# A decoder layer on one core: a second product in the first sweep over x, and the last attention groups placed between other blocks

## The chip, the cores and the metric

The kernel runs on one core of a Trainium2 chip. The metric is the device time of one execution in microseconds (us), and lower is better. Before the change the median of three runs is 1527.37 us (1514.87 to 1532.27).

## The reference, cut to what matters

One layer of a decoder with 256 tokens and 2048 channels, in fp32. It has three sub-layers: token mixing, attention into 256 memory tokens, and a gated MLP with a short convolution. The MLP takes the larger half of the time. The change touches token mixing alone:

```python
proj = x @ w_in[l]
(sq, sk, sv, gq, gk, gv, gz, gb, ga, gate_swa, gate_gdn) = split_columns(proj, IN_WIDTHS)
y_swa = swa_attention(sq, sk, sv, swa_sinks[l], rel_bias) @ w_br_swa[l]       # 16 heads, window 128
y_gdn = gated_deltanet(gq, gk, gv, gz, gb, ga, ...) @ w_br_gdn[l]             # 8 heads of 128
mixed = sigmoid(gate_swa) * y_swa + sigmoid(gate_gdn) * y_gdn
...
z = silu(gz).reshape(b, s, GDN_HEADS, GDN_HEAD_DIM)   # in gated_deltanet: 1024 columns of z
o = o * rsqrt(mean(o*o) + 1e-6) * norm_w
return (o * z)
```

The delta rule also needs, for each head, a short causal convolution with SiLU over k, q and v, and a matrix of decays `exp(gc_i - gc_j)` from the cumulated gates.

## The kernel before, in words

**Numbers.** Each fp32 operand is split into a high and a low part (`split`, L60: ScalarE writes the high part, VectorE subtracts), and each product is made of hi*hi, hi*lo and lo*hi. So every weight that lands from memory passes through ScalarE (`whi`, L61) and VectorE (`wlo`, L58) before TensorE may use it. Weights arrive in tiles `raw` of up to 1024 columns on the sync queue (`load_raw`, L64 to L67). There are four buffers each of `raw`, `whi` and `wlo`. `load_w` (L69) gives its load and split a higher priority than the code around it, by 40 places or another number (`ahead`).

**Two forms of product.** `prod_a` (L81) keeps the weights stationary and streams x: 16 k-tiles, each a matmul of 512 columns and one of 256. One block of 128 output channels is 32 matmuls from two raw tiles. `prod_b` (L97) keeps x stationary and streams the weights: per k-tile and half of the tokens three matmuls of n columns. It can be called for a part of the k-tiles (`k_from`, `k_to`) and go on into the same PSUM tiles (`ps`).

**Order of the work.** Tile, the framework, puts each engine's instructions into one list, by the order of the program and the priorities; each engine then runs its list in that order. The first part of the program is:

- L158 to L160: eight matmuls on zeros.
- L186 to L189, the first k sweep: for six ranges of k-tiles (1, 1, 2, 4, 4, 4) `load_x` loads x (on ScalarE's queue, L169) and splits it, and `prod_b` multiplies it with `wS`. Those 400 columns are v of the attention, the two gates and the first 256 columns of z.
- L312 to L317: blocks of the attention's k and q with `prod_a`, the position bias through GpSimd's DMAs, scores and softmax of head group 0 (`swa_probs(0)`).
- L319 to L341: cumulated gates, a DMA that spreads them over the partitions (`dgd`, `dcr`), and the decays: 16 VectorE instructions (L339) and 16 exponentials on ScalarE (L340, L341).
- L343 to L357: head groups 1 to 3 of the attention in turn with the rest of z: `wZ0` (512 columns) in two halves of k, and `wZ1` (256 columns). `swa_probs(g)` makes scores in four PSUM banks and the softmax; `swa_out(g)` makes 12 transposes of the probabilities (L300), three copies (L301), 6 matmuls with v (L306) and two splits (L310). The banks of these steps come from one pool of four (`bank`, tag `sm`); the products use another pool of four (tag `mm`).
- L428 to L434: the delta rule's heads, three blocks each for k, q and v (`gdn_block`, L381: a `prod_a`, the convolution on VectorE, SiLU), and the scores of the head before.

After that come the triangular inverse on VectorE beside the attention's output products, the merge, the memory attention and the MLP.

Of the kernel before, what the change touches and what calls it, by code (L numbers as in the profile page):

```python
# [14 lines left out]
P = 128  # L15
# [18 lines left out]
def tile_layer(ctx: ExitStack, tc: tile.TileContext, a, out):  # L34
# [19 lines left out]
    def stt(o, i0, s, i1, op0, op1, **k):  # L54
        nc.vector.scalar_tensor_tensor(o, i0, s, i1, op0=op0, op1=op1, **k)  # L55
# [36 lines left out]
    def evac_a(ps, dst):  # L92
        hl = tp.tile([P, T], F32, tag="hl", name="hl")
        nc.scalar.copy(hl, ps[:, T:])  # L94
        tt(dst, ps[:, :T], hl, ALU.add)

    def prod_b(w, kt, n, xs, tail=0, ps=None, k_from=0, k_to=None, ahead=AHEAD, homes={}):  # L97
        pss = ps or [pb.tile([P, 512], F32, tag="mm", name="mm") for _ in range(2)]
        step = min(kt, U // n)
        pend = []  # L100

        def emit(items, order):
            for h in order:
                for kk, wh, wl in items:
                    o = pss[h][:, :n]
                    xh, xl = xs(kk, h)
                    mm(o, xh, wh, kk == 0, False)
                    mm(o, xh, wl, False, False)
                    mm(o, xl, wh, False, kk == kt - 1)

        for k0 in range(k_from, k_to or kt, step):
            ks = min(step, (k_to or kt) - k0)
            wh, wl = load_w(w[:, k0 * n:(k0 + ks) * n], ks, n, ahead, homes.get(k0))
            for k in range(ks):
                it = (k0 + k, wh[:, k, :], wl[:, k, :])
                if it[0] >= kt - tail:
                    pend.append(it)
                else:
                    emit([it], (0, 1))
        if pend:  # L120
            emit(pend, (0, 1))
        return pss

    def halves(x):
        def f(kk, h):
            v = x(kk)
            return v[:, 0, h * P:(h + 1) * P], v[:, 1, h * P:(h + 1) * P]
        return f
# [37 lines left out]

    def load_x(k0, n):
        raw = xst[k0 // 8].rearrange("p q (k t) -> p (q k) t", t=T)[:, k0 % 8:k0 % 8 + n, :]
        nc.scalar.dma_start(raw, a["xT"][:, k0 * T:(k0 + n) * T].rearrange("p (k t) -> p k t", t=T))  # L169
        x, c = xhl[k0 // 8], slice(k0 % 8, k0 % 8 + n)  # L170
        split(x[:, c, 0, :], x[:, c, 1, :], raw)

# [7 lines left out]
    def z_gate(c0, n, h, src):  # L180
        zc = zn[:, h, c0:c0 + n]
        nc.scalar.activation(zc, src, AF.Silu)
        z3 = zc.rearrange("p (h d) -> p h d", d=P)
        tt(z3, z3, nrm.unsqueeze(1).broadcast_to([P, n // P, P]), ALU.mult, nc.gpsimd)

    pss = None  # L186
    for k0, n in ((0, 1), (1, 1), (2, 2), (4, 4), (8, 4), (12, 4)):
        load_x(k0, n)
        pss = prod_b(a["wS"], KT, 400, halves(xs), ps=pss, k_from=k0, k_to=k0 + n, ahead=20)  # L189
    nc.sync.dma_start(sml, a["sml"].partition_broadcast(P))  # L190
    nc.sync.dma_start(cst, a["cst"])
    nc.sync.dma_start(nrm, a["nrm"].partition_broadcast(P))
# [1 line left out]
        nc.scalar.copy(svg[:, h, :], ps[:, :144])  # L194
    for h, ps in enumerate(pss):
        z_gate(0, 256, h, ps[:, 144:400])


    rd = dp.tile([16, RELW], F32, name="rd")
# [8 lines left out]
    def sm16(name):  # L208
        return cp.tile([P, 2, 8], F32, name=name)
# [49 lines left out]
    def swa_probs(g):  # L259
        b = biasg[g // 2][:, 4 * (g % 2):4 * (g % 2) + 4, :]  # L260
        s = S[:, g % 2]
        s0, s1 = s[:, :, 0:128], s[:, :, 128:384]
        for j in range(2):
            r = slice(64 * j, 64 * j + 64)
            hh = slice(2 * j, 2 * j + 2)
            for sd, bd, tq, nk in ((s1, b, slice(128, 256), 256), (s0, b[:, :, 128:256], slice(0, 128), 128)):
                ps = bank()[:, :2 * nk].rearrange("p (h k) -> p h k", k=nk)
                for i in range(2):
                    q = qhl[r, g % 2, i, :, tq]
                    mm(ps[:, i, :], q[:, 0, :], khl[r, 0, :nk], True, False)  # L270
                    mm(ps[:, i, :], q[:, 0, :], khl[r, 1, :nk], False, False)
                    mm(ps[:, i, :], q[:, 1, :], khl[r, 0, :nk], False, True)
                stt(sd[:, hh, :], ps, 0.125, bd[:, hh, :], ALU.mult, ALU.add)
        mx = tp.tile([P, 2, 4], F32, tag="mx", name="mx")
        nc.vector.reduce_max(mx[:, 0, :], s0, axis=AX.X)
        nc.vector.reduce_max(mx[:, 1, :], s1, axis=AX.X)
        sk = sinkb[:, 4 * g:4 * g + 4].unsqueeze(1).broadcast_to([P, 2, 4])
        tt(mx, mx, sk, ALU.max)
        nm = tp.tile([P, 2, 4], F32, tag="nm", name="nm")
        nc.vector.tensor_scalar_mul(nm, mx, -1.0)  # L280
        l = tp.tile([P, 2, 4], F32, tag="l", name="l")
        for h in range(4):
            nc.scalar.activation(s0[:, h, :], s0[:, h, :], AF.Exp, bias=nm[:, 0, h:h + 1],
                                 accum_out=l[:, 0, h:h + 1])
            nc.scalar.activation(s1[:, h, :], s1[:, h, :], AF.Exp, bias=nm[:, 1, h:h + 1],
                                 accum_out=l[:, 1, h:h + 1])
        tt(mx, sk, nm, ALU.add)
        nc.scalar.activation(mx, mx, AF.Exp)
        tt(l, l, mx, ALU.add)
        nc.vector.reciprocal(l, l)  # L290
        for bl, sd in ((0, s0), (1, s1)):
            tt(sd, sd, l[:, bl, :].unsqueeze(2).broadcast_to(list(sd.shape)), ALU.mult)

    def swa_out(g):
        s = S[:, g % 2]
        pt = slot(f"E{4 + g % 2}", [P, 4, RELW], F32, "pt")
        for c in range(3):
            ps = bank()
            for h in range(4):
                pe_t(ps[:, h * P:(h + 1) * P], s[:, h, c * P:(c + 1) * P])  # L300
            nc.scalar.copy(pt[:, :, c * P:(c + 1) * P], ps.rearrange("p (h k) -> p h k", k=P))  # L301
        po = bank().rearrange("p (b i q) -> p b i q", b=2, i=2)
        for bl, c, t, st, sp_ in ((0, 0, 0, True, True), (1, 1, 0, True, False), (1, 2, 1, False, True)):
            for j in range(2):
                r = slice(64 * j, 64 * j + 64)
                mm(po[r, bl], sv[:, t, r], pt[:, 2 * j:2 * j + 2, c * P:(c + 1) * P], st, sp_)  # L306
        o = osT[g // 2][:, 2 * (g % 2):2 * (g % 2) + 2]
        for bl in range(2):
            q = slice(bl * P, bl * P + P)
            split(o[:, :, 0, q], o[:, :, 1, q], po[:, bl])  # L310
# [22 lines left out]
    dcr = e8[:, 3:7, :].rearrange("p a (b t) -> p (a b) t", t=P)  # L333
    nc.gpsimd.dma_start(dgd, gd.partition_broadcast(P))
    nc.gpsimd.dma_start(dcr, gd[1].partition_broadcast(P))
    for h in range(8):
        for hf in range(2):
            d = dgd[:, hf, h, :]
            stt(d, d, ngc[:, hf, h:h + 1], msk, ALU.add, ALU.add)  # L339
        nc.scalar.activation(dcr[:, h, :], dcr[:, h, :], AF.Exp, bias=suf[:, 0, h:h + 1])  # L340
        nc.scalar.activation(dgd[:, :, h, :], dgd[:, :, h, :], AF.Exp)  # L341

    swa_q(2)  # L343
    zps = prod_b(a["wZ0"], KT, 512, halves(xs), k_to=8)
    swa_probs(1)
# [4 lines left out]
        z_gate(256, 512, h, zps[h])  # L350
    swa_probs(2)
    swa_out(1)
    for h, ps in enumerate(prod_b(a["wZ1"], KT, 256, halves(xs))):
        z_gate(768, 256, h, ps[:, :256])
    swa_probs(3)
    swa_out(2)
    swa_out(3)  # L357

    def transpose_split(src, kt, dst):
# [6 lines left out]
            split(hi, lo, ps)  # L366


    nc.sync.dma_start(gcw, a["gcw"])
    nc.sync.dma_start(fcw, a["fcw"])  # L370
    nc.sync.dma_start(lnT, a["lnT"])
    cvr = []
    for i in range(3):
        c = cp.tile([P, 3 + T], F32, name=f"cv{i}")
        nc.vector.memset(c[:, 0:3], 0.0)
        cvr.append(c)

    ua = [slot(f"T{i}", [P, 4, 768], F32, f"ua{i}") for i in range(2)]
    vp = slot("E1", [P, 2, 8, P], F32, "vp")
    ks, ck, sq, cq = sm16("ks"), sm16("ck"), sm16("sq"), sm16("cq")  # L380
    def gdn_block(h, j, dst):  # L381
        blk = 3 * h + j
        cv = cvr[blk % 3]
        evac_a(prod_a(a["wA"][blk], xs), cv[:, 3:])
        ca = tp.tile([P, T], F32, tag="ca", name="ca")
        nc.vector.tensor_scalar_mul(ca, cv[:, 3:3 + T], gcw[:, blk, 3:4])
        for w in (2, 1, 0):
            stt(ca, cv[:, w:w + T], gcw[:, blk, w:w + 1], ca, ALU.mult, ALU.add)
        nc.scalar.activation(dst, ca, AF.Silu)

    def gdn_scores(h, kq, vt):
        kh = tp.tile([P, 2, T], F32R, tag="t2", name="kh", bufs=3)
        kl = tp.tile([P, 2, T], F32R, tag="t2", name="kl", bufs=3)
# [31 lines left out]
        for hf in range(2):  # L425
            nc.scalar.activation(vp[:, hf, h, :], ps[:, hf * P:(hf + 1) * P], AF.Copy,
                                 scale=sq[:, hf, h:h + 1])
    kqv = slot("E6", [P, 2, 3, T], F32, "kqv")  # L428
    for h in range(8):
        for j in range(3):  # L430
            gdn_block(h, j, kqv[:, h % 2, j, :])
            if j == 0 and h:
                gdn_scores(h - 1, kqv[:, (h - 1) % 2, 0:2, :], kqv[:, (h - 1) % 2, 2, :])
    gdn_scores(7, kqv[:, 1, 0:2, :], kqv[:, 1, 2, :])  # L434
# [436 lines left out]
```

## Time and profile before

| | us |
|---|---|
| median of three runs | 1527.37 |
| lowest, highest | 1514.87, 1532.27 |
| the profiled execution | 1521.04 |
| its span, first to last instruction | 1519.3 |
| TensorE busy in it | 1497.7 |

A profile shows one execution. TensorE has two rows, PE for matmuls and PEld for the loading of the stationary operand. An engine's busy time counts overlapping instructions once. A wait names the instruction that ended it. "Clock" is the share of TensorE's full clock that was granted.

### The profile page before, as it was taken

What the parts mean: (1) busy time and instruction counts of PE and PEld (TensorE: products, weight loads), DVE (VectorE), ACT (ScalarE), POOL (GpSimd) and SP (SyncE); (2) the same over time, 40 slices, a digit from 0 to 9 for tenths busy, and PEclk for the clock granted to TensorE, in tenths of its full rate; (3) what the DMA queues carried; (4) which work ended last, traced back from release to release, by engine and by line L of the source; (5) the groups of instructions that cost most, each with busy time, mean ns of one, the idle gap of its engine ahead of it and who ended that gap; (6) DMA issues with size and microseconds to landing.
All of it is one profiled execution on the core that took longest, in us unless ns stands there. A gap on an engine that the chain in (4) does not pass through costs nothing.

```text
span 1519.3 us, 21775 instructions
## 1 busy us (share of the span) xinstructions
PE 1497.7 (99%) x8182; PEld 1279.1 (84%) x8182; DVE 1094.2 (72%) x1803; ACT 749.3 (49%) x1153; POOL 57.0 (4%) x93
## 2 busy tenths in 40 slices
PE   7999999999999999999999999999999999999998
PEld 6878888888898888888878888888888888888886
DVE  4876888869956666659579777887777787455455
ACT  5566654554446555436455454444445444343332
POOL 0101002030001000000000000000000000000000
PEclk9999999999999999999999999999999999999999
DMA  7853455585554656765644555555555557666663
GB/s 255 229 177 124 153 171 178 169 241 191 186 192 144 190 190 192 246 189 169 219 139 153 191 191 187 192 187 193 190 190 191 188 192 242 195 196 192 187 203 118
DMA packets 79845, 285.75 MB, mean 188 GB/s; under 512 B 9659, under 2 KB 10876, under 8 KB 78460
## 3 DMA queue, kind: packets, MB, share of 16 engines
q1 hardware_dynamic: 75404, 267.55, 54.9%
q0 software_dynamic: 3040, 14.06, 3.0%
q10 hardware_dynamic: 1296, 2.75, 0.5%
q8 instruction: 64, 1.05, 0.3%
q14 instruction: 41, 0.34, 0.1%
HBM read 281.80 MB, written 2.52 MB: 187 GB/s over the span
## 4 chain that ended last, share of the span: by engine, by line
PE 67%; DVE 1%; ACT 0%; POOL 0%; issue 0%; DVEq 0%
PE mm L46 66%; PE sm L46 1%; PE sm L151 1%; DVE wlo L58 0%; POOL rv L58 0%; DVE xn L55 0%; DVE st L617 0%; ACT whi L61 0%; DVE xn L592 0%; DVE zn L55 0%; DVE xn L58 0%; ACT xn L590 0%; DVE x2hl L58 0%; ACT ptm L677 0%; DVE mv L577 0%
## 5 line engine op out<-in xcount | busy, mean ns | idle before, releaser
L58 DVE TENSOR_TENSOR wlo<-raw,whi 128x1024 fp32r<-128x1024 f32 (+3 forms) x505 | 611.9, 1213 | 299.0 <-ACT whi L61 297.0
L61 ACT CAST whi<-raw 128x1024 fp32r<-128x1024 f32 (+3 forms) x505 | 526.5, 1044 | 575.8 <-PE mm L46 417.6
L46 PE MATMUL mm<-x2hl,whi 128*128 128x512 f32 x1376 | 477.6, 394 | 0.6 <-DVE x2hl L58 0.6
L46 PE MATMUL mm<-x2hl,wlo 128*128 128x256 f32 x1376 | 381.3, 277 | 0.0
L46 PE MATMUL mm<-xhl,whi 128*128 128x512 f32 x1040 | 369.1, 398 | 0.0
L46 PEld LDWEIGHTS mm<-x2hl,whi 128*128 128x128 f32 x1376 | 257.9, 188 | 60.6 <-DVE x2hl L58 0.8
L46 PE MATMUL mm<-xhl,wlo 128*128 128x256 f32 x1040 | 290.8, 280 | 0.0
L46 PEld LDWEIGHTS mm<-x2hl,wlo 128*128 128x128 f32 x1376 | 258.2, 188 | 0.1
L46 PEld LDWEIGHTS mm<-xhl,whi 128*128 128x128 f32 x1040 | 195.3, 188 | 47.8 <-issue 2.4
L46 PEld LDWEIGHTS mm<-xhl,wlo 128*128 128x128 f32 x1040 | 196.0, 188 | 0.0
L46 PE MATMUL mm<-whi,hT_E 128*128 128x512 f32 x384 | 119.3, 389 | 0.0
L46 PE MATMUL mm<-whi,hT_T 128*128 128x512 f32 x288 | 89.4, 389 | 0.0
L55 DVE SCALAR_TENSOR_TENSOR ca<-cv,fcw,ca 128x256 f32<-128x256 f32 x172 | 83.0, 482 | 4.3
L46 PEld LDWEIGHTS mm<-whi,hT_E 128*128 128x128 f32 x384 | 72.1, 188 | 15.1
L46 PE MATMUL mm<-whi,mixT 128*128 128x512 f32 x256 | 79.0, 389 | 0.0
L46 PE MATMUL mm<-wlo,hT_E 128*128 128x512 f32 x192 | 74.7, 389 | 0.0
L94 ACT COPY hl<-mm 128x256 f32<-128x256 f32 x191 | 68.8, 360 | 0.0
L46 PEld LDWEIGHTS mm<-whi,hT_T 128*128 128x128 f32 x288 | 54.1, 188 | 11.3
L46 PE MATMUL mm<-whi,xhl 128*128 128x400 f32 (+2 forms) x192 | 51.9, 352 | 7.0 <-ACT xhl L61 6.4
L58 DVE TENSOR_TENSOR cv<-mm,hl 128x256 f32<-128x256 f32 x110 | 46.0, 418 | 15.1 <-ACT hl L94 15.1
L46 PEld LDWEIGHTS mm<-whi,mixT 128*128 128x128 f32 x256 | 48.0, 188 | 10.0
L46 PE MATMUL mm<-wlo,hT_T 128*128 128x512 f32 x144 | 56.0, 389 | 0.0
(254 smaller groups left out, 1604.3 us busy)
## 6 DMA issues: line engine op xcount, KB each, us to landing
raw<-in_wU_dram SPq DMA_DIRECT2D x172, 512.0 KB, 4.4
raw<-in_wD_dram SPq DMA_DIRECT2D x84, 512.0 KB, 4.3
raw<-in_wA_dram SPq DMA_DIRECT2D x66, 512.0 KB, 4.0
raw<-in_wGS_dram SPq DMA_DIRECT2D x32, 512.0 KB, 4.3
raw<-in_wGG_dram SPq DMA_DIRECT2D x32, 512.0 KB, 4.4
raw<-in_wMO_dram SPq DMA_DIRECT2D x32, 512.0 KB, 4.4
raw<-in_wBS_dram SPq DMA_DIRECT2D x16, 512.0 KB, 4.1
raw<-in_wBG_dram SPq DMA_DIRECT2D x16, 512.0 KB, 4.3
```

What stands on the lines that cost most here:

```text
L46: nc.tensor.matmul(o, l, r, start=start, stop=stop)
L55: nc.vector.scalar_tensor_tensor(o, i0, s, i1, op0=op0, op1=op1, **k)
L58: (eng or nc.vector).tensor_tensor(o, i0, i1, op=op)
L61: nc.scalar.copy(dst_hi, src)
L94: nc.scalar.copy(hl, ps[:, T:])
L151: nc.tensor.transpose(o, i, ident)
```

## The change

- The first k sweep takes nine ranges of k-tiles (1, 1, 2, then six of 2). After each range of the `wS` product the same range of the `wZ1` product is made, into two PSUM tiles of its own. The two tiles of the `wS` product come from the pool `sm`. The product `wZ1` between the attention groups is gone.
- The loads of x are issued on the sync queue.
- `swa_probs(3)` comes behind `swa_out(1)`; then the k and q blocks of the delta rule's first head, `swa_out(2)`, its v block, and `swa_out(3)`.
- The 16 + 16 instructions of the decays stand behind the first head's k and q blocks in the program.

```diff
     def load_x(k0, n):
-        nc.scalar.dma_start(raw, a["xT"][:, k0 * T:(k0 + n) * T].rearrange("p (k t) -> p k t", t=T))
+        nc.sync.dma_start(raw, a["xT"][:, k0 * T:(k0 + n) * T].rearrange("p (k t) -> p k t", t=T))
...
-    pss = None
-    for k0, n in ((0, 1), (1, 1), (2, 2), (4, 4), (8, 4), (12, 4)):
+    pss = [bank() for _ in range(2)]
+    zps = [pb.tile([P, 512], F32, tag="mm", name="mm") for _ in range(2)]
+    for k0, n in ((0, 1), (1, 1), (2, 2), (4, 2), (6, 2), (8, 2), (10, 2), (12, 2), (14, 2)):
         load_x(k0, n)
-        pss = prod_b(a["wS"], KT, 400, halves(xs), ps=pss, k_from=k0, k_to=k0 + n, ahead=20)
+        prod_b(a["wS"], KT, 400, halves(xs), ps=pss, k_from=k0, k_to=k0 + n, ahead=20)
+        prod_b(a["wZ1"], KT, 256, halves(xs), ps=zps, k_from=k0, k_to=k0 + n, ahead=20)
...
+    for h, ps in enumerate(zps):
+        z_gate(768, 256, h, ps[:, :256])
...
-    for h in range(8):
-        for hf in range(2):
-            d = dgd[:, hf, h, :]
-            stt(d, d, ngc[:, hf, h:h + 1], msk, ALU.add, ALU.add)
-        nc.scalar.activation(dcr[:, h, :], dcr[:, h, :], AF.Exp, bias=suf[:, 0, h:h + 1])
-        nc.scalar.activation(dgd[:, :, h, :], dgd[:, :, h, :], AF.Exp)
-
     swa_q(2)
...
     swa_out(1)
-    for h, ps in enumerate(prod_b(a["wZ1"], KT, 256, halves(xs))):
-        z_gate(768, 256, h, ps[:, :256])
     swa_probs(3)
-    swa_out(2)
-    swa_out(3)
...
+    kqv = slot("E6", [P, 2, 3, T], F32, "kqv")
+    gdn_block(0, 0, kqv[:, 0, 0, :])
+    gdn_block(0, 1, kqv[:, 0, 1, :])
+    for h in range(8):
+        for hf in range(2):
+            d = dgd[:, hf, h, :]
+            stt(d, d, ngc[:, hf, h:h + 1], msk, ALU.add, ALU.add)
+        nc.scalar.activation(dcr[:, h, :], dcr[:, h, :], AF.Exp, bias=suf[:, 0, h:h + 1])
+        nc.scalar.activation(dgd[:, :, h, :], dgd[:, :, h, :], AF.Exp)
+
+    swa_out(2)
+    gdn_block(0, 2, kqv[:, 0, 2, :])
+    swa_out(3)
...
     for h in range(8):
         for j in range(3):
-            gdn_block(h, j, kqv[:, h % 2, j, :])
+            if h:
+                gdn_block(h, j, kqv[:, h % 2, j, :])
```

What the lists of the engines look like is shown at three places. First the start of the sync engine's list, which issues the loads of `raw` and now those of x; before:

```order
L66 DMA raw<-in_wS_dram 128x400 x2
L66 DMA raw<-in_wS_dram 128x800 x4
L190 DMA sml<-in_sml_dram 128x32
L66 DMA raw<-in_wS_dram 128x800 x3
L191 DMA cst<-in_cst_dram 128x512
L66 DMA raw<-in_wA_dram 128x1024
```

and after the change:

```order
L66 DMA raw<-in_wS_dram 128x400
L66 DMA raw<-in_wZ_dram 128x256
L66 DMA raw<-in_wS_dram 128x400
L169 DMA xst_104<-in_xT_dram 128x256
L66 DMA raw<-in_wZ_dram 128x256
L169 DMA xst_104<-in_xT_dram 128x256
L169 DMA xst_104<-in_xT_dram 128x512
L66 DMA raw<-in_wS_dram 128x800
L66 DMA raw<-in_wZ_dram 128x512
```

The loads of x stand among those of the weights, x of the first k-tile fourth, and nothing else is issued ahead of the last range; `cst` and the first `wA` tile follow behind it.

Second the decays in VectorE's list (`dgd`), among the low parts of the weights (`wlo`); before:

```order
L58 TENSOR_TENSOR wlo<-raw,whi 128x1024
L55 SCALAR_TENSOR_TENSOR dgd<-dgd,ngc,cst 128x128 x16
L58 TENSOR_TENSOR wlo<-raw,whi 128x1024
L58 TENSOR_TENSOR qk<-mm,hl 128x256
L58 TENSOR_TENSOR wlo<-raw,whi 128x1024
```

and after:

```order
L58 TENSOR_TENSOR wlo<-raw,whi 128x1024
L58 TENSOR_TENSOR qhl<-qk,qhl 128x256
L55 SCALAR_TENSOR_TENSOR dgd<-dgd,ngc,cst 128x128 x3
L58 TENSOR_TENSOR wlo<-raw,whi 128x1024
L55 SCALAR_TENSOR_TENSOR dgd<-dgd,ngc,cst 128x128 x7
L58 TENSOR_TENSOR wlo<-raw,whi 128x1024
L55 SCALAR_TENSOR_TENSOR dgd<-dgd,ngc,cst 128x128 x6
```

The 16 instructions stand in three pieces with a `wlo` between them, and start two `wlo` later.

Third TensorE's list from the end of `swa_out(1)` (`sm<-pt,swakv`) on; before, `wZ1` followed, here its first rows:

```order
L151 MATMUL sm<-cst,S 128x128 x12
L46 MATMUL sm<-pt,swakv 64x256 x6
L46 MATMUL mm<-whi,xhl_102 128x256
L46 MATMUL mm<-wlo,xhl_102 128x256
L46 MATMUL mm<-whi,xhl_102 128x256 x2
```

and now the scores of group 3 (`sm<-khl,qhl`) follow, and then 64 matmuls of two delta-rule blocks, of which the first two are shown:

```order
L46 MATMUL sm<-pt,swakv 64x256 x6
L46 MATMUL sm<-khl,qhl 128x256 x6
L46 MATMUL sm<-khl,qhl 128x128 x6
L46 MATMUL sm<-khl,qhl 128x256 x6
L46 MATMUL sm<-khl,qhl 128x128 x6
L46 MATMUL mm<-xhl_102,whi 128x512
L46 MATMUL mm<-xhl_102,wlo 128x256
```

Behind those 64 come the 12 transposes of `swa_out(2)`.

## Rows read from the trace of the kernel before

**Rows 1.** The page, part 1: busy us (share of the span) xinstructions.
```profile
PE 1497.7 (99%) x8182; PEld 1279.1 (84%) x8182; DVE 1094.2 (72%) x1803; ACT 749.3 (49%) x1153; POOL 57.0 (4%) x93
```
**Rows 2.** Windows; columns: stretch, length, busy by engine, clock, DMA share, GB/s.
```profile
0.00:34.40 34.40, 25.79 (x107) 21.39 (x107) 16.94 (x26) 16.99 (x23) 0.20 (x4) 0.95 0.78 254
34.40:165.00 130.60, 126.71 (x760) 105.77 (x760) 94.45 (x167) 82.03 (x180) 14.12 (x19) 0.97 0.56 172
165.00:1519.30 1354.30, 1345.17 (x7319) 1151.94 (x7317) 982.84 (x1612) 650.32 (x952) 42.67 (x70) 1.00 0.59 188
```
**Rows 3.** Waits from 0 to 34 us: total us, times, longest.
```profile
ACT xhl L61 <- DMA xst<-in_xT_dram: 10.3, 4, 5.7
...
PE mm L46 <- ACT xhl L61: 6.4, 4, 3.0
```
**Rows 4.** Timeline of PE: start us, us, instruction, count [idle before].
```profile
5.16 0.54 PE L46 MATMUL mm<-whi,xhl 128*128 128x400 f32 x1
...
25.08 0.63 PE L46 MATMUL mm<-whi,xhl 128*128 128x400 f32 x2 [0.63 <-DVE xhl L58]
...
33.62 0.81 PE L46 MATMUL sm<-oh,ohr 33*16 33x384 f32 x2
34.36 0.50 PE L46 MATMUL mm<-xhl,whi 128*128 128x512 f32 x1
...
62.82 1.38 PE L46 MATMUL sm<-khl,qhl 64*128 64x256 f32 x11
```
**Rows 5.** Timeline of ACT, its DMA queue: the last load of x.
```profile
15.93 0.34 ACTq L169 DMA_DIRECT2D xst<-in_xT_dram  x1
```
**Rows 6.** DMA issues from 0 to 30 us: count, KB each, median us to landing.
```profile
raw<-in_wS_dram SPq DMA_DIRECT2D x7, 400.0 KB, 5.6
...
xst<-in_xT_dram ACTq DMA_DIRECT2D x3, 512.0 KB, 8.6
raw<-in_wS_dram SPq DMA_DIRECT2D x2, 200.0 KB, 3.5
```
**Rows 7.** Windows, columns as in rows 2: a starved stretch of the first sweep.
```profile
15.00:20.00 5.00, 2.98 (x8) 2.54 (x9) 2.18 (x2) 1.04 (x1) 0.00 (x0) 0.69 0.91 301
```
**Rows 8.** Groups by shape, 0 to 34 us: busy us, mean ns | idle before.
```profile
L58 DVE TENSOR_TENSOR wlo<-raw,whi 128x800 fp32r<-128x800 f32 x7 | 6.7, 987 | 1.7 <-ACT whi L61 1.7
...
L58 DVE TENSOR_TENSOR xhl<-xst,xhl 128x512 fp32r<-128x512 f32 x1 | 0.7, 693 | 2.4 <-ACT xhl L61 2.4
...
L61 ACT CAST whi<-raw 128x1024 fp32r<-128x1024 f32 x3 | 3.2, 1051 | 2.9 <-DMA raw<-in_wA_dram 1.7 <-PE mm L46 1.1
```
**Rows 9.** Timeline of PE: `wZ1` begins, and `swa_out(2)` with what follows it.
```profile
129.63 0.38 PE L46 MATMUL mm<-whi,xhl 128*128 128x256 f32 x1
...
141.34 0.50 PE L46 MATMUL sm<-khl,qhl 64*128 64x256 f32 x2
...
145.18 0.66 PE L151 MATMUL sm<-cst,S 128*128 128x128 f32 x4 [0.23 <-DVE S L55]
```
**Rows 10.** Waits of PE from 34 to 165 us: total us, times, longest.
```profile
PE sm L151 <- DVE S L55: 2.5, 3, 1.2
PE mm L46 <- DVE wlo L58: 1.3, 1, 1.3
```
**Rows 11.** Timeline of DVE: the decays' 16 instructions.
```profile
79.33 4.29 DVE L55 SCALAR_TENSOR_TENSOR dgd<-dgd,ngc,cst 128x128 f32<-128x128 f32 x16 [0.76 <-DMA dgd<-gd]
```
**Rows 12.** Timelines of ACT and DVE behind `swa_out(1)`.
```profile
130.15 1.28 ACT L283 ACT_TABLE_LOAD   x1
...
135.07 0.34 ACT L61 CAST osT<-sm 128x256 fp32r<-128x256 f32 x1
...
135.81 1.82 DVE L58 TENSOR_TENSOR S<-S,l 128x512 f32<-128x512 f32 x2
```
**Rows 13.** Windows, columns as in rows 2: around `swa_out(0)` and `swa_out(1)`.
```profile
81.00:99.00 18.00, 15.54 (x84) 11.23 (x83) 14.65 (x27) 10.09 (x21) 0.00 (x0) 0.91 0.61 194
121.00:130.00 9.00, 7.88 (x53) 5.55 (x52) 6.22 (x10) 3.95 (x8) 2.51 (x2) 0.81 0.40 130
```

More of the change, by code (lines that the diff above doesn't have):

```diff
@@ L352, in tile_layer @@
     swa_out(1)
-    for h, ps in enumerate(prod_b(a["wZ1"], KT, 256, halves(xs))):
-        z_gate(768, 256, h, ps[:, :256])
     swa_probs(3)
-    swa_out(2)
-    swa_out(3)
-    def transpose_split(src, kt, dst):
-        for k0 in range(0, kt, 2):
-            ps = bank().rearrange("p (k t) -> p k t", t=T)
-            for k in range(2):
-                for h in range(2):
-                    pe_t(ps[:, k, h * P:(h + 1) * P], src(k0 + k, h))
-            hi, lo = dst(k0)
-            split(hi, lo, ps)
     nc.sync.dma_start(gcw, a["gcw"])
@@ L376, in tile_layer @@
         cvr.append(c)
-    ua = [slot(f"T{i}", [P, 4, 768], F32, f"ua{i}") for i in range(2)]
-    vp = slot("E1", [P, 2, 8, P], F32, "vp")
     ks, ck, sq, cq = sm16("ks"), sm16("ck"), sm16("sq"), sm16("cq")
@@ L389, in gdn_block, with transpose_split @@
         nc.scalar.activation(dst, ca, AF.Silu)
+    kqv = slot("E6", [P, 2, 3, T], F32, "kqv")
[10 more added lines that the diff above has]
+    swa_out(3)
+    def transpose_split(src, kt, dst):
+        for k0 in range(0, kt, 2):
+            ps = bank().rearrange("p (k t) -> p k t", t=T)
+            for k in range(2):
+                for h in range(2):
+                    pe_t(ps[:, k, h * P:(h + 1) * P], src(k0 + k, h))
+            hi, lo = dst(k0)
+            split(hi, lo, ps)
+    ua = [slot(f"T{i}", [P, 4, 768], F32, f"ua{i}") for i in range(2)]
+    vp = slot("E1", [P, 2, 8, P], F32, "vp")
     def gdn_scores(h, kq, vt):
@@ L427, in gdn_scores @@
                                  scale=sq[:, hf, h:h + 1])
-    kqv = slot("E6", [P, 2, 3, T], F32, "kqv")
     for h in range(8):
         for j in range(3):
-            gdn_block(h, j, kqv[:, h % 2, j, :])
+            if h:
+                gdn_block(h, j, kqv[:, h % 2, j, :])
             if j == 0 and h:
```

## The prediction, made before the changed kernel ran

> **What bounds the kernel now.** I read the busy shares first. TensorE is busy for 1497.7 us of a span of 1519.3 [rows 1]; no other engine comes near. So the time is TensorE's work plus the little it loses, and a change that keeps the matmuls can win back only losses. The table by stretches shows where they lie [rows 2]: idle is length less PE's busy time, so 8.6 us in the first 34.4, 3.9 us up to 165, and 9.1 us in all the rest, which the change doesn't touch. A busy PE can also be a slow one, and the clock column, a mean over the two levels of 1.2 and 2.4 GHz, shows it: 0.95 and 0.97 of the full clock in the first two stretches, 1.00 behind them.
>
> Then the waits of the first stretch: TensorE waits 6.4 us for the high part of x, and ScalarE, which makes it, 10.3 us for x to land [rows 3]. The reason stands in ScalarE's queue: the last load of x is issued at 15.93, behind casts that the engine has to do first [rows 5]. The sweep runs from 5.16 to 33.62 [rows 4]. Unhindered it needs less: 47 matmuls of 400 columns take 8.54 us from 25.08 to 33.62, 0.182 each, and 96 of them 17.5. The stage lasts 28.5, so 11.0 us are lost in it, to waiting and to the lower clock, 0.69 in one stretch [rows 7].
>
> Last the waits of the second stretch: 2.5 us for transposes that wait for a PSUM bank, and 1.3 us for a `wlo` [rows 10]. The latter is the decays' doing: their 16 instructions hold VectorE for 4.29 us [rows 11], and the `wlo` behind them comes late. Around `swa_out(0)` and `swa_out(1)` the clock falls, after a wait and short matmuls; 18 us at 0.91 and 9 us at 0.81 [rows 13] cost 18 x 0.09 = 1.6 and 9 x 0.19 = 1.7 us.
>
> **The first sweep.** The 96 matmuls of `wZ1` leave their old place, from 129.63 to 141.34 [rows 9]: 11.7 us go there, 0.122 each. They come back in the sweep, where TensorE was waiting. How long is the sweep now? Three bounds:
>
> - TensorE: 17.5 + 11.7 = 29.2 us of matmuls. x of the first k-tile is now the fourth load that the sync engine issues; at 0.34 us for an issue [rows 5] it starts some 1.0 later, so I put the first matmul at 6.0 instead of 5.16. The end is at 35.2 if TensorE never waits again.
> - The bytes: x 2.1 MB, `wS` 3.3 and `wZ1` 2.1 are 7.5 MB. At the 301 GB/s of a full stretch [rows 7] that is 25 us, and with some 3.5 us to the first landing [rows 6] and the work on the last range, one of 3.65 us, the end is near 32. Not the bound.
> - The ring of buffers. Four `raw` tiles now hold two ranges (one `wS` and one `wZ1` tile each). A range of two k-tiles is 12 x 0.182 + 12 x 0.122 = 3.65 us for TensorE and 0.99 + 0.69 + 0.69 = 2.4 us for VectorE, with `wZ1` taken like x, both 512 columns [rows 8]. A tile is loaded anew only when VectorE has freed it; then an issue, the landing and the splitting follow, until the next range but one is ready. With a landing of 5.6 us [rows 6] that is 5.6 + 0.8 for two issues + 2.4 = 8.8 us for two ranges, 4.4 each. The first two ranges, of one k-tile, end at 6.0 + 3.65 = 9.65; seven more of 4.4 end at 40.4.
>
> With the short landing of 3.5 us [rows 6] the ring gives 3.35 a range and TensorE bounds again. So the end lies between 35.2 and 40.4; I take the middle, 37.8, since nothing but these loads is in flight now (the order shows `cst` and `wA` behind them). It was 33.6. The sweep's net is 11.7 - 4.2 = 7.5 us won, between 4.9 and 10.1. What follows should not be late: two more SiLU and two more multiplies on GpSimd stand there, but the `wS` tiles are finished 12 x 0.122 = 1.5 us before the sweep ends, and ScalarE starts on them then.
>
> Here a rule of the Trainium skill speaks against the change: "DMA: Bandwidth & Descriptors", section "Rules for kernel authors", asks for transfers of 1 MiB or more for bandwidth, and its section on the anatomy of a DMA gives each one some 2.0 us of fixed cost. The change cuts x from six loads to nine and adds nine for `wZ1`. An estimate from that page, if fixed costs added up: 12 x 2.0 = 24 us, and the sweep would lose 24 - 11.7 = 12 us instead of winning. The rows don't show them added: the 400 KB loads already fill the engines to 0.91 [rows 7], and 200 KB land in 3.5 us against 5.6. I stay with the sum.
>
> **The decays.** In VectorE's list they come two `wlo` later and in three pieces, so a `wlo` waits for at most seven of them, 7/16 of 4.29 = 1.9 us, not for all. The wait of 1.3 us can go (bounds 0 and 1.3). I take 1.0. Nobody needs the decays before the scores of head 0, which come after `swa_out(3)`.
>
> **The attention groups.** `swa_probs(3)` follows `swa_out(1)` at once. Its fourth bank was the one of `swa_out(1)`'s result, but it writes only the half that the first split reads, so it does not queue behind the second cast, at 135.07 [rows 12]. Then 64 matmuls of two delta-rule blocks cover the softmax: 160 matmuls take 28.5 us from 34.36 to 62.82 [rows 4], so 64 take 11.4. Call the end of `swa_out(1)` zero (129.7 before). Scores end at 2.6, blocks at 14.0. ScalarE: table load to 1.7, exponentials of group 2 to 5.4 [rows 12]; VectorE scales group 2 (1.82 us) until about 8; exponentials of group 3, again 3.6 us, until 12; then the copy of block 0, three `whi` of 1.05 [rows 8], the copy of block 1, and only then the copies of `swa_out(2)`, some 0.6 each. The first copy is ready at about 16.2. TensorE's transposes end near 15.1 and two more matmuls at 15.5, so it waits 0.7 to 1.0 us there; the 0.23 of before [rows 9] goes. Net +0.7, bounds -0.2 and +3. Queued behind that wait are the v block and `swa_out(3)`, the rest of which is covered.
>
> The clock: the stall at `swa_out(1)` stays and so does its dip. A third dip behind the wait at `swa_out(2)` would cost 1.7 us; even odds, so +0.9 (bounds -3.3, if both old dips go, and +3.4).
>
> **Sum.** -7.5 - 1.0 + 0.7 + 0.9 = -6.9, say -7. On the profiled execution, 1521.04 us (span 1519.3 and 1.7 around it), that gives 1514. The three runs shown lie at 1514.87, 1527.37 and 1532.27, so this execution is on their fast side; the middle of all four is 1524.2, and I predict 1517. A difference of under 1%, 15 us, can hardly be told from none with runs that spread over 17 us.
>
> **Rivals.** (1) The ring holds the sweep up. If every load takes the 8.6 us of the large x loads [rows 6], a range takes (8.6 + 0.8 + 2.4) / 2 = 5.9 us, the sweep ends at 9.65 + 41.3 = 51, which is 17.3 later than before against 11.7 saved; with the other terms (-1.0 + 0.7 + 0.9) the kernel is 6 us slower, 1530. It decides from a landing of 7.0 us on, where a range takes 5.1 and the sweep eats its own gain. Against it: those 8.6 us were measured on 512 KB loads beside weights on a second queue. Chance 0.1. This is also where the skill's rule would lead. (2) Everything goes well: the sweep ends at 35.2, the decays' wait goes wholly and both dips of the clock go, since the work falls otherwise: -10.1 - 1.3 - 3.3 = -14.7, 1509. For it speaks that TensorE's waits in the sweep are nearly all for x. Chance 0.2. (3) The gain of the sweep is there, but behind `swa_out(1)` it is given back: ScalarE's list holds the copies of `swa_out(2)` and `swa_out(3)` behind casts, +3 at each and two dips of 1.7: -7.5 - 1.0 + 6 + 3.4, about +1, 1525. Against it: 11.4 us of blocks lie between. Chance 0.15.
>
> **Numbers.** The forecast has 0.55, the rivals 0.1, 0.2 and 0.15. The range 1505 to 1530 takes in all of these and a few us of the runs' own spread at the fast end. Faster by over 1% needs nearly rival 2 in full or a fast set of runs: 0.18. Slower by over 1% is out of reach of every case but a rival 1 with a slow set: 0.05. Within 1%: 0.77.
>
> **What would show it.** Right: the first `prod_a` matmul (34.36 before) starts at 37 to 40, PE's idle time ahead of it falls under 5 us, the wait for the `xhl` casts is no longer TensorE's longest there; no wait for `wlo` near 85; a wait of about 1 us at `swa_out(2)`; all beyond it as before, some 7 us earlier. Wrong: the first `prod_a` matmul after 45, or a wait of over 3 us between `swa_probs(3)` and the first delta-rule scores.

## The result, and the profile after

| | before | after |
|---|---|---|
| median us (22 runs each) | 1527.47 | 1517.78 |
| lowest to highest | 1514.87 to 1532.27 | 1506.57 to 1523.25 |
| profiled execution, us (span) | 1521.04 (1519.3) | 1518.57 (1516.7) |

The ratio is 0.9943, 95% interval 0.9922 to 0.9963: 8.7 us less, between 5.7 and 11.9. The forecast was 1517 and a change within 1%. The part of the page with the busy times, which answers to [rows 1]:

```profile
PE 1500.9 (99%) x8182; PEld 1284.2 (85%) x8182; DVE 1095.2 (72%) x1811; ACT 747.2 (49%) x1159; POOL 57.5 (4%) x93
```

The table by stretches of the changed kernel, cut as in [rows 2] (stretch, length, busy time by engine, clock, DMA share, GB/s), and below it a stretch of its own, the two of [rows 13], and all from 77 us to the end of the changed code:

```profile
0.00:34.40 34.40, 31.97 (x181) 30.64 (x182) 19.60 (x36) 19.14 (x32) 0.20 (x4) 1.00 0.86 268
34.40:165.00 130.60, 127.20 (x745) 105.83 (x743) 100.58 (x182) 84.64 (x187) 14.09 (x19) 0.99 0.59 184
165.00:1516.70 1351.70, 1341.70 (x7260) 1147.76 (x7259) 975.02 (x1595) 643.42 (x941) 43.24 (x70) 1.00 0.58 187
...
70.00:77.00 7.00, 6.74 (x31) 5.71 (x32) 6.87 (x14) 2.36 (x11) 0.51 (x1) 0.76 0.96 289
81.00:99.00 18.00, 17.95 (x100) 14.88 (x99) 16.77 (x32) 12.83 (x27) 0.00 (x0) 1.00 0.77 249
121.00:130.00 9.00, 7.88 (x59) 6.13 (x57) 6.91 (x8) 5.76 (x8) 2.51 (x2) 1.00 0.51 167
77.00:165.00 88.00, 85.86 (x510) 70.37 (x508) 69.33 (x123) 61.81 (x144) 5.44 (x5) 1.00 0.47 154
```

TensorE idles 2.4 us in the first stretch instead of 8.6. The dips of the clock, as I call its stretches at the lower level, around `swa_out(0)` and `swa_out(1)` are gone (from 77 us on it is 1.00), and one near 72 is new. Rows of TensorE's timeline of the changed kernel (start, us, instruction, idle before):

```profile
6.21 0.70 PE L46 MATMUL sm<-whi,xhl 128*128 128x400 f32 x1 [0.85 <-ACT xhl L61]
...
37.21 0.81 PE L46 MATMUL sm<-oh,ohr 33*16 33x384 f32 x2
37.96 0.50 PE L46 MATMUL mm<-xhl,whi 128*128 128x512 f32 x1
...
66.41 2.59 PE L46 MATMUL sm<-khl,qhl 64*128 64x256 f32 x24
70.26 0.62 PE L46 MATMUL sm<-gg,cst 128*128 128x16 f32 x4 [1.26 <-DVE S L55]
...
128.04 0.66 PE L151 MATMUL sm<-cst,S 128*128 128x128 f32 x4 [1.12 <-DVE S L55]
...
146.03 0.65 PE L46 MATMUL sm<-pt,swakv 128*64 128x256 f32 x4 [0.16 <-ACT pt L305]
...
155.84 0.65 PE L46 MATMUL sm<-pt,swakv 128*64 128x256 f32 x4 [0.81 <-ACT pt L305]
...
163.03 0.40 PE L46 MATMUL sm<-kh 128*128 128x512 f32 x1
```

Behind 6.21 no wait is left in the sweep. Before the gate matmuls (70.26) VectorE is late with the first S; its timeline there:

```profile
68.38 1.23 DVE L58 TENSOR_TENSOR wlo<-raw,whi 128x1024 fp32r<-128x1024 f32 x1 [0.52 <-PE sm L46]
69.52 0.68 DVE L55 SCALAR_TENSOR_TENSOR S<-sm,bias 128x512 f32<-128x512 f32 x1
```

Put side by side, the starts of the same work give a ledger:

| start of | before | after | difference | what happened since the mark above |
|---|---|---|---|---|
| first `prod_a` | 34.36 | 37.96 | +3.6 | `wZ1`'s 11.7 us came, 8.1 were won |
| gate matmuls | 65.34 | 70.26 | +4.9 | a new wait, 1.26 |
| `swa_probs(1)` | 90.25 | 95.06 | +4.8 | the `wlo` wait (1.30) goes, a dip comes |
| `swa_probs(2)` | 121.24 | 123.31 | +2.1 | a wait (1.16) and a dip go |
| `swa_probs(3)` | 141.34 | 130.07 | -11.3 | a dip goes, `wZ1`'s 11.7 go |
| first delta-rule scores | 173.35 | 163.03 | -10.3 | waits 0.16 + 0.81 instead of 0.23; 0.2 has no cause that I found |

So 10.3 us are won by the point where the changed code ends, but the spans differ by 2.6. The rest is lost in matmuls that the change doesn't touch; the last section has it.

Landings of the loads issued in the first 30 us of the changed kernel (count, KB each, median us), against [rows 6]:

```profile
raw<-in_wS_dram SPq DMA_DIRECT2D x7, 400.0 KB, 3.7
xst<-in_xT_dram SPq DMA_DIRECT2D x7, 256.0 KB, 4.5
raw<-in_wZ_dram SPq DMA_DIRECT2D x7, 256.0 KB, 4.3
```

### The profile page after: what moved, and what is told of

The parts are those of the page before. It is cut to its first block, busy times and chain, and to the rows that moved or that the text cites. A ratio compares the mean times of both kernels' runs of the same rounds, so it can differ in the third digit from the quotient of the medians.

```text
span 1516.7 us, 21812 instructions
## 1 busy us (share of the span) xinstructions
PE 1500.9 (99%) x8182; PEld 1284.2 (85%) x8182; DVE 1095.2 (72%) x1811; ACT 747.2 (49%) x1159; POOL 57.5 (4%) x93
## 4 chain that ended last, share of the span: by engine, by line
PE 68%; DVE 1%; ACT 0%; POOL 0%; issue 0%; DVEq 0%; ACTq 0%
PE mm L46 67%; PE sm L46 1%; PE sm L151 1%; DVE wlo L58 0%; POOL rv L58 0%; DVE xn L55 0%; DVE st L625 0%; ACT whi L61 0%; DVE xn L600 0%; DVE zn L55 0%; DVE xn L58 0%; ACT xn L598 0%; ACT pm L670 0%; DVE x2hl L58 0%; ACT ptm L685 0%
## 5 line engine op out<-in xcount | busy, mean ns | idle before, releaser
L58 DVE TENSOR_TENSOR wlo<-raw,whi 128x1024 fp32r<-128x1024 f32 (+2 forms) x510 | 612.9, 1203 | 308.2 <-ACT whi L61 306.7
L61 ACT CAST whi<-raw 128x1024 fp32r<-128x1024 f32 (+2 forms) x510 | 527.0, 1035 | 560.0 <-PE mm L46 390.5
L46 PE MATMUL mm<-x2hl,whi 128*128 128x512 f32 x1376 | 486.6, 399 | 0.6 <-DVE x2hl L58 0.6
L46 PE MATMUL mm<-x2hl,wlo 128*128 128x256 f32 x1376 | 386.5, 281 | 0.0
L46 PEld LDWEIGHTS mm<-whi,hT_T 128*128 128x128 f32 x288 | 54.1, 188 | 11.3
L46 PE MATMUL mm<-wlo,mixT 128*128 128x512 f32 x128 | 49.8, 389 | 0.0
```

The lines of the kernel that those rows point to most:

```text
L46: nc.tensor.matmul(o, l, r, start=start, stop=stop)
L58: (eng or nc.vector).tensor_tensor(o, i0, i1, op=op)
L61: nc.scalar.copy(dst_hi, src)
```

## The experiments

Times are medians with the ratio to the kernel before, measured beside it; 10 to 12 runs, 7 for the two raw buffers. The kernel before, measured beside them, had medians from 1521.0 to 1527.3, so times of different experiments are compared by their ratios. "Scores" are the first delta-rule scores. The changed sweep itself ends by up to 1.2 us earlier or later from profile to profile (first `prod_a` at 36.73 to 37.96, where nothing in it was edited).

**The sweep alone.** The kernel before with the new loop of the first sweep, x on the sync queue, and this:

```diff
-    for h, ps in enumerate(prod_b(a["wZ1"], KT, 256, halves(xs))):
-        z_gate(768, 256, h, ps[:, :256])
```

> The new sweep (x on the sync queue, the z product's last 256 columns inside it), with the decays and the attention groups in the order of the kernel before. First theory, that the wZ1 matmuls had also been the cover for the softmax of groups 2 and 3: the first prod_a matmul starts at 38 as in the changed kernel, but behind swa_out(1) TensorE has only the 2.6 us of swa_probs(3) left to do before swa_out(2). Group 2 is scaled some 8 us after the end of swa_out(1) and group 3 some 14 us after it, so it waits about 5 us at swa_out(2) and 3 at swa_out(3): of the 8 us won in the sweep nothing is left, the first delta-rule scores start at 171 to 175 (173.35 before, 163.03 in the changed kernel) and the time is that of before within 3 us. Rival, that the sweep is the whole of the gain and the order behind it is worth nothing: waits of under 1 us at both, first delta-rule scores at 164 to 166, and a time 7 to 9 us under before.

Measured: first `prod_a` at 37.10, scores at 165.37, 1521.63 us, ratio 0.997 (0.9954 to 0.9986). The first theory fell: the one wait at `swa_out(2)` was 1.21 us, and `swa_out(3)` had none. Where I had counted an uncovered softmax, the trace shows 18 matmuls of delta-rule blocks; the scheduler had pulled them forward by itself. The rival is right on the start of the scores and half right on the time, which fell by 4.6 us (2.1 to 7.0) and not by 7 to 9. The sweep gives 8.0 of the 10.3 us at the scores.

**The order alone.** The changed kernel with the sweep of before, and `wZ1`'s loop behind `swa_out(1)` again.

> The kernel before with the second half of the change alone: decays behind two delta-rule blocks, and these blocks between swa_probs(3), swa_out(2) and swa_out(3); the sweep and wZ1's place between the groups are those of before. First theory: the order wins nothing but the decays' wait of 1.3 us, and brings about 0.7 at swa_out(2) and swa_out(3); the first delta-rule scores start at 172 to 174 (173.35 before) plus or minus 1.7 for each dip of the clock that comes or goes, and the time is within 3 us of before. Rival, that the order itself wins what the sweep does not: first scores at 168 or earlier and a time 4 us or more under before.

Measured: scores at 169.86, 1527.44 us, ratio 0.9996 (0.9966 to 1.0026). The first `prod_a` was 1.9 us earlier here, in a sweep that wasn't edited; of the 3.5 us at the scores 1.6 are left for the order. No measurable gain by itself, as the first theory has it. In the times the two halves give 4.6 and 0.6 us, against 8.7 together; the intervals are too wide to say whether the rest comes of having both. What nine ranges instead of six are worth by themselves no run shows.

**x on the sync queue alone**, in the kernel before:

```diff
-        nc.scalar.dma_start(raw, a["xT"][:, k0 * T:(k0 + n) * T]...
+        nc.sync.dma_start(raw, a["xT"][:, k0 * T:(k0 + n) * T]...
```

> The kernel before with one edit: x's six loads are issued by the sync engine. First theory, that TensorE's waits in the first sweep came from x being issued late, behind ScalarE's casts: the first prod_a matmul starts at 27 to 31 instead of 34.36 (28.5 us of sweep less some 3 to 7 of its 11 lost ones), and the time falls by 3 to 7 us. Rival, that the transfers themselves were the limit (the 512 KB loads of x need 8.6 us each, and two queues are then worth more than one): the start stays at 33 to 36 and the time within 2 us of before.

Measured: first `prod_a` at 27.24, 7.1 us earlier, so it was x's place on ScalarE's queue that made TensorE wait. The last load of x was now issued at 12.76 instead of 15.93, and those of 512 KB landed in 6.6 us instead of 8.6; this run doesn't separate the two. But the time is 1528.32, ratio 1.0003 (0.9977 to 1.0028): most of the gain is gone before the scores (170.77, 2.6 earlier). Two waits for `whi` (0.98 and 0.67) come at once behind the sweep, and two stretches of low clock: 0.57 in 61 to 65, behind a new wait at the gate matmuls, and 0.57 in 91 to 99, where TensorE waits 2.27 us for S instead of 1.16. TensorE's timeline in this kernel:

```profile
27.24 0.50 PE L46 MATMUL mm<-xhl,whi 128*128 128x512 f32 x1
...
92.74 1.97 PE L151 MATMUL sm<-cst,S 128*128 128x128 f32 x8 [2.27 <-DVE S L55]
```

I read it so: the sweep's idle time had hidden the lateness of ScalarE and VectorE; filled with `wZ1`, it is work that goes from elsewhere for good.

**x back on ScalarE's queue**, in the changed kernel:

> The changed kernel with x's nine loads back on ScalarE's queue. First theory: ScalarE issues x of the later ranges only behind casts that wait for other landings, so TensorE waits for x again, 2 to 5 us in all; the first prod_a matmul starts at 40 to 43 instead of 37.96, and the time is 2 to 5 us above the changed kernel's. Rival, that the smaller pieces of x and TensorE's longer work per range are enough, and the queue plays no part: the first matmul starts at 5.2 to 5.5 instead of 6.21 and the first prod_a at 37 to 38.

Measured: first `prod_a` at 41.35, scores at 164.65, 1522.04 us (0.9982, 0.9958 to 1.0005). The size is the first theory's, its reason is half of it: one wait of 2.84 us, at 13.15, and a dip behind it. In the timelines of TensorE and ScalarE, the wait, the issue of the third load of x, and the cast that waits for it:

```profile
13.15 0.63 PE L46 MATMUL sm<-whi,xhl 128*128 128x400 f32 x2 [2.84 <-ACT whi L61]
```

```profile
5.54 0.33 ACTq L169 DMA_DIRECT2D xst<-in_xT_dram  x1
...
11.72 0.62 ACT L61 CAST xhl<-xst 128x512 fp32r<-128x512 f32 x1 [4.78 <-DMA xst<-in_xT_dram]
```

That load was issued behind ScalarE's first casts, 2.0 us later than in the changed kernel (3.5), and its cast began 6.2 us after the issue instead of 4.0. The longer landing is general here: among the loads issued in the first 30 us a 256 KB load of x took 6.2 us in the median and one of `wZ1` 5.6 on two queues, against 4.5 and 4.3 on one.

**Two raw buffers** for the sweep's weights instead of four:

```diff
+        raw = slot(f"T{two[0] % 2}", [P, U], F32, "raw2")
```

> The changed kernel with two raw buffers instead of four for the weights of the first sweep (they take turns in T0 and T1, which are free at that time); nothing else is changed. It tests the ring formula behind the bound of 40.4 and rival 1. By that formula two buffers hold one range, so a range takes a landing of 3.7 to 4.5 us (the changed kernel's own) + 0.8 for the issues + 2.4 for the splits = 6.9 to 7.7 us; the first two ranges end near 10.5, seven more at 59 to 64, and the time rises by 20 to 26 us over the changed kernel. If the ring plays no part because ScalarE's and VectorE's order holds the loads back anyway, the first prod_a matmul stays at 38 to 40 and the time is that of the changed kernel.

Measured: first `prod_a` at 55.20, 1532.17 us, ratio 1.0045 (1.0011 to 1.008), 16 above the changed kernel beside it (20 to 26 were expected). TensorE's waits up to 56 us in this kernel (us in all, times, longest):

```profile
PE sm L46 <- ACT whi L61: 10.1, 6, 3.4
```

The ring can bound the sweep, so rival 1 was a real mechanism; but seven ranges took 44.7 us from 10.5 on, 6.4 each, where the formula gave 6.9 to 7.7. It adds the splits to the landing one after the other; perhaps they overlap in part, which I didn't look into. Nor is the buffer count all that differs: the four ordinary buffers are now free, so `cst` and four loads of `wA` are issued between 10 and 22 us, in the middle of the sweep, and three dips of the clock fall into it.

**Early gates** (run e7). `ngc`, `suf` and `gcr` between the two query blocks of group 1:

> The changed kernel with one edit: the three gate matmuls (ngc, suf, gcr) stand between the two query blocks of group 1 and no longer behind swa_probs(0). Theory: their wait of 1.26 us came from needing a fifth bank of pool sm while VectorE still held the four of swa_probs(0), and the dip of the clock at 71.9 followed from it. Both go: no wait for S before 80, the z product ends at 92 to 94 (95.06 in the changed kernel), the first delta-rule scores start at 160 to 161.8 (163.03), and the time is 1 to 3 us under the changed kernel's. Rival, that the wait only moves (to the same matmuls waiting for gg or to the next user of the bank) and the dip comes anyway: the z product ends at 95 or later and the first scores start at 162.5 to 164.

Measured: scores at 163.04, 1516.03 us, ratio 0.9943 (0.9915 to 0.9971). The rival is right on the scores, though not on the z product. The wait at the gates is gone and `swa_probs(1)` starts at 90.89, 4.2 us earlier, of which 1.2 come from the sweep; then TensorE waits at `swa_out(0)`, and the clock falls there. Its timeline in this kernel, and the stretch by windows:

```profile
94.07 0.91 PE L151 MATMUL sm<-cst,S 128*128 128x128 f32 x4 [0.59 <-DVE S L55]
...
96.44 1.97 PE L151 MATMUL sm<-cst,S 128*128 128x128 f32 x8 [1.47 <-DVE S L55]
```

```profile
93.00:102.00 9.00, 6.94 (x34) 4.47 (x33) 5.91 (x12) 5.38 (x16) 0.00 (x0) 0.62 0.49 146
```

`swa_probs(2)` starts at 123.31, to the hundredth where it did in the changed kernel.

**Early gates and the first x on ScalarE's queue.**

> The kernel of e7 with the first two loads of x (one k-tile each) on ScalarE's queue, the other seven on the sync engine's. Theory: x of the first k-tile need not stand behind three loads of weights; the first matmul starts at 5.5 (as with all x on ScalarE) instead of 6.21, nothing else in the sweep is late, and the first prod_a starts at 37.0 to 37.6 instead of 37.96; 0.4 to 0.9 us come on top of e7's gain. Rival, that the second range's weights land later for it: the first matmul is early but a wait of as much follows before 14, and the first prod_a stays at 37.9 or later.

Measured: first matmul at 5.43, a wait of 1.18 at 11.19, first `prod_a` at 37.85, scores at 165.28; 1514.22 us, ratio 0.9947 (0.992 to 0.9974). The rival is right.

**The changed kernel again.**

> The changed kernel once more, without an edit, beside the other three: what of its profile repeats. If the waits are the program's own, the wait at the gate matmuls is again 1.0 to 1.5 us, the first prod_a starts within 1 us of 37.96 and the first delta-rule scores within 2 us of 163.03 (a dip of the clock more or less). If the pace of the w_up matmuls (0.347 or 0.353 us for a pair of 512 and 256 columns) is drawn anew in each execution, that stretch takes 479 or 488 us whatever the kernel; if it belongs to the kernel, it takes 488 again.

Measured: first `prod_a` at 37.09, the wait at the gates 1.29, scores at 163.32; 1516.11 us, ratio 0.9941 (0.9912 to 0.997). The waits are the program's own; the dip at the gates is 6.8 us long here instead of 3.4. The `w_up` matmuls took 487.9 us again (last section).

**Decays back** in their old place, the rest as changed:

> The changed kernel with the decays back where they stood before (behind the gate matmuls, ahead of swa_q(2)); TensorE's list is the changed kernel's, only VectorE's and ScalarE's differ: all 16 stand in one piece ahead of a wlo. Theory of the prediction: the wait of TensorE for that wlo comes back, 0.5 to 1.5 us (1.30 in the kernel before), and with it at most a dip of the clock; the z product ends 0.5 to 1.5 us later than in the changed kernel. But the run with early gates showed that TensorE, where it comes early to swa_out(0), waits there for VectorE's S: if that holds here too, most of the delay is made up at swa_out(0), and the first delta-rule scores start at 162 to 165 (163.03 and 163.32 in the two profiles of the changed kernel), the time within 2 us of the changed kernel's 1516 to 1518. Rival, that the decays' move carries a good part of the gain: first scores at 166 or later and a time of 1520 or more.

Measured: the wait for `wlo` is back, 1.38; `swa_out(0)` waits 0.98 more, scores at 165.21, 1515.59 us, ratio 0.9957 (0.9929 to 0.9984). TensorE's timeline:

```profile
90.94 0.50 PE L46 MATMUL mm<-wlo,xhl 128*128 128x512 f32 x1 [1.38 <-DVE wlo L58]
...
100.53 1.25 PE L151 MATMUL sm<-cst,S 128*128 128x128 f32 x8 [0.98 <-DVE S L55]
```

The scores start between the two theories, and the time is the first one's. The delay isn't made up: the move is worth 1.9 to 2.2 us at the scores, less than the runs can tell.

**Late gates**, behind `swa_probs(3)`:

> The changed kernel with the gate matmuls and all that hangs on them (the copies, the broadcast through DRAM, the decays) behind swa_probs(3), ahead of the first delta-rule block. Theory: the gates' wait of 1.26 to 1.29 us at 69 goes without a successor, because the 16 instructions of the decays (4.3 us of VectorE) and their exponentials on ScalarE no longer stand between the softmax of groups 0 and 1, so VectorE frees the banks for swa_out(0) in time. No wait over 0.6 us between 60 and 100; the z product ends at 90.5 to 92 (95.06), swa_probs(2) starts at 120.5 to 122 (123.31 and 123.68), the first delta-rule scores start at 160 to 161.5, with a new wait of up to 1 us at the gates behind swa_probs(3); the time is 1 to 3 us under the changed kernel's. Rival, that the decays only move their price to the blocks of head 0 and the last groups: swa_probs(2) starts at 121 as well, but waits of 1.5 us or more come at swa_out(2), swa_out(3) or for a wlo behind 133, and the first scores start at 162.5 or later.

Measured: `swa_probs(2)` at 120.39, 2.9 us earlier, as the theory has it; scores at 167.28, 4 later; 1524.0 us, ratio 0.9989 (0.9957 to 1.002). The rival is right, by more than it said. In the timelines of VectorE and TensorE, eleven decays in one piece stand ahead of a `wlo` that TensorE needs:

```profile
147.88 2.98 DVE L55 SCALAR_TENSOR_TENSOR dgd<-dgd,ngc,cst 128x128 f32<-128x128 f32 x11
150.77 2.36 DVE L58 TENSOR_TENSOR wlo<-raw,whi 128x1024 fp32r<-128x1024 f32 x2
...
152.05 0.58 PE L46 MATMUL mm<-xhl,wlo 128*128 128x256 f32 x1 [5.29 <-DVE wlo L58]
```

**Gates in the middle**, right behind `swa_out(0)`:

> The changed kernel with the gate matmuls and the broadcast behind them at a third place, right behind swa_out(0); the decays are written where the changed kernel has them, and fall in four pieces between the wlo of swa_q(3) and of the z product's second half, where VectorE was busy for 13.1 of 23 us. Theory: there the decays find room, so the first half runs as with late gates (no wait for S at 69, z product's first half ends at 91 to 92.5, swa_out(0) a good 2 us earlier than in the changed kernel), and the 5.29 us wait that late gates caused behind swa_probs(3) is gone. swa_probs(2) starts at 121 to 122 (1.0 us of gate matmuls now stands ahead of it; 123.31 and 123.68 in the changed kernel, 120.39 with late gates), the first delta-rule scores at 160.5 to 162 (163.03 and 163.32), and the time is about 2 us under the changed kernel's, which runs of this spread will hardly tell. Rival, that VectorE's list is the limit of this whole stretch wherever the decays stand: a wait for wlo or at swa_out(1) of 1.5 us or more, and first scores at 163 or later.

Measured: `swa_probs(2)` at 119.30, 4 us earlier (1.0 of it from the sweep), with hardly a wait from 60 to 120; then 3.22 us at `swa_out(1)` and the clock at 0.51 for 14 us; scores at 166.29, 1513.95 us, ratio 0.9955 (0.993 to 0.9981). The rival is right again. Two windows of this kernel, then VectorE's timeline:

```profile
60.00:120.00 60.00, 59.94 (x340) 50.14 (x339) 47.92 (x80) 37.51 (x90) 3.95 (x7) 1.00 0.63 204
125.00:139.00 14.00, 12.46 (x53) 9.92 (x54) 10.71 (x21) 6.21 (x21) 0.00 (x0) 0.51 0.13 43
```

```profile
123.67 2.21 DVE L58 TENSOR_TENSOR wlo<-raw,whi 128x1024 fp32r<-128x1024 f32 x1 [1.17 <-ACT whi L61]
125.81 1.01 DVE L55 SCALAR_TENSOR_TENSOR S<-sm,bias 128x512 f32<-128x512 f32 x2
```

In VectorE's list a `wlo` stands ahead of the S that frees the bank, and its `whi` is late on ScalarE. No version beat the changed kernel by more than the runs' spread: the five ratios of the changed kernel, early gates, early gates with the first x, decays back and middle gates lie between 0.9941 and 0.9957, though the scores start between 163.0 and 166.3.

## Why the prediction was right

- **The sweep** (-7.5): measured -8.1, and -9.0 in the second profile. The rel matmul starts at 37.21 by the forecast's 37.8, inside 35.2 to 40.4. But the middle was right for another reason than the one given: with landings of 3.7 to 4.5 us the ring didn't bind, TensorE did, without a wait. What it lost against 35.2 was mostly a slow start: up to 10.3 a matmul of 400 columns took 0.54 us, behind that 0.34. The 14 matmuls from 6.21 to 10.32 took 4.1 us; at the later pace they take 8 x 0.182 + 6 x 0.122 = 2.2. I take that for the clock, because 0.54 is also what this matmul took in the kernel before at 18 to 20 us, at a clock of 0.50; but the clock column has 1.00 for this start, so it isn't shown. The forecast had no term for it.
- **The decays** (-1.0): the wait of 1.3 went, and putting them back costs 1.9 to 2.2 at the scores. Mis-sized: a second wait, at `swa_out(0)`, hangs on it.
- **The attention groups** (+0.7): 0.16 + 0.81 - 0.23 = +0.74. The size is right by luck, since the place isn't: the wait came at `swa_out(3)`, which the forecast called covered, and `swa_out(2)` waited 0.16 instead of 0.7 to 1.0.
- **The clock** (+0.9): wrong in sign. In the profiles, outside the sweep, two dips went (1.7 us each by the forecast's price) and one came, -1.7. Over all executions the mean granted clock is 0.9962 before (104 runs) and 0.9988 after (34): 0.0026 x 1520 = 4 us, the sweep's dip of before included and waits too, so an upper bound. "The stall at `swa_out(1)` stays and so does its dip" failed: the stall stayed (1.12), the dip didn't.
- **Not in the sum**: the wait of 1.26 at the gate matmuls, with a dip behind it. They take the bank of pool `sm` that the scores of `swa_probs(0)` took first, and VectorE empties it late, at 69.52 behind a `wlo`. The forecast said "What follows should not be late", and looked only at the work right behind the sweep; I hadn't asked what comes late next in the first group.
- **The rivals.** The ring (1) is real with two buffers and absent with four: the landings were far from 7.0. That is also the answer to the rule of 1 MiB in the page "DMA: Bandwidth & Descriptors" of the Trainium skill (section "Rules for kernel authors"): the first stretch, now made almost wholly of loads of 128 to 400 KB, moved 268 GB/s against 254 before. The forecast's 24 us of fixed cost, an estimate from the same page of the Trainium skill, borrowed a figure that the page's section on the anatomy of a DMA gives for transfers issued by GpSimd, while these are issued by the sync engine. No such cost shows here: behind 6.21 TensorE has no wait in the sweep. Of the all-well case (2) the sweep's part came nearly in full (8.1 to 9.0 of 10.1), the decays' wait went wholly and both dips went; the new wait at the gates and its dip took 3.0 of that back. Rival 3, the gain given back at the last groups, didn't happen in the changed kernel, but it did with late gates.

The terms as measured are -8.1 - 1.3 + 0.7 - 1.7, and for what wasn't in the sum + 1.3 at the gates and - 1.2 at `swa_out(0)`, where the old wait went: -10.3, as in the ledger. The forecast said -6.9; most of the difference is the clock's term. The runs say -8.7, with an interval that holds both. That 1517 was hit so closely is partly luck: it was counted from 1524.2, and the kernel before has its median at 1527.5, 3 us higher, which made up for a gain forecast too small.

## What to carry to other kernels

Here idle time was won for good when work from elsewhere filled it; taking the idle time away alone (x on the sync queue) moved the wait behind the sweep and won nothing that the runs could tell. Where TensorE meets the same two slower engines again and again, removing one wait (early, middle, late gates) brings TensorE earlier to the next meeting, and there it waited as long or longer (1.26 us at the gates, against 2.1, 3.2 and 5.3 further on): look at what frees the next bank before promising a gain. A scheduler that fills gaps by itself makes part of a hand-made order unnecessary.

## What was not expected of the hardware

**Two paces of one matmul at the same clock.** The same 1376 pairs of matmuls in the `w_up` stage (the MLP's first product), by the page's costliest groups, first of the changed kernel, then of the kernel with the decays back, whose list for TensorE is the same:

```profile
L46 PE MATMUL mm<-x2hl,whi 128*128 128x512 f32 x1376 | 486.6, 399 | 0.6 <-DVE x2hl L58 0.6
L46 PE MATMUL mm<-x2hl,wlo 128*128 128x256 f32 x1376 | 386.5, 281 | 0.0
```

```profile
L46 PE MATMUL mm<-x2hl,whi 128*128 128x512 f32 x1376 | 477.6, 394 | 0.6 <-DVE x2hl L58 0.6
L46 PE MATMUL mm<-x2hl,wlo 128*128 128x256 f32 x1376 | 381.3, 277 | 0.0
```

From the first to the last of them 487.9 us pass in the one and 478.9 in the other, at a granted clock of 1.00 and with one wait of 0.6. The kernel before had the shorter time in its profile, and in another stage, the attention's output products, a slower pace by 2.5 us (129.7 against 127.2); with some tenths elsewhere that is why 10.3 us became 2.6. The two have the same list, so that doesn't decide it; of all thirteen profiles four have 478.9 and nine 487.9. Whether the execution does is not shown: both profiles of the changed kernel have 487.9, as they would if the pace were the kernel's, and no kernel was profiled at both paces. The runs of one kernel, 1506.57 to 1523.25 for the changed one, leave room for it. What decides it is open. Comparing two single profiles by their spans would have given 2.6 us, where the runs give 8.7; the ledger of starts isn't touched by it.

**A wait of 1.12 us with and without a dip.** At `swa_out(1)` the kernels before and after wait 1.12 us each; before, the clock falls behind it (0.81 in [rows 13]), after it stays at 1.00. What decides that is open too.
